# Where the side sums of the modulation vector run in a one-core two-block kernel

## The chip, the cores and the metric

One core of one Trainium2 chip runs the whole program. The metric is the device time of one execution in microseconds (us); the time before is the median of three executions. The engines are named as in the profile: PE is TensorE's matmul, PEld its weight load, DVE is VectorE, ACT is ScalarE, POOL is GpSimd, and SP is the queue from which nearly all DMA loads are issued, in program order.

## What is computed

The reference is a stack of two layers over 256 tokens of width 2048: an RWKV-7 mixer with a convolutional feed-forward, then a layer with windowed attention, a gated recurrence and an MLP. What the change touches is the modulation vector of the first layer:

```python
mod = jax.nn.silu(c) @ ada_w + ada_b                       # (2048) @ (2048, 6*2048)
sh_m, sc_m, g_m, sh_f, sc_f, g_f = jnp.split((mod + ada_table[layer])[:, None, :], N_MOD, axis=-1)
h = _rms(x, norm_mix_pre[layer]) * (1 + sc_m) + sh_m
y, v_first = _rwkv7_mix(h, ...)                            # ends with y @ w_o
x = x + g_m * _rms(y, norm_mix_post[layer])
h = _rms(x, norm_ffn_pre[layer]) * (1 + sc_f) + sh_f
f = _conv_ffn(h, ...)
```

`sh_m` and `sc_m` are needed at the very start. The columns of `g_m`, `sh_f` and `sc_f` (3 x 2048) are needed only at the end of the mixer; they are the work that moves.

## The kernel before

All weights come from HBM as 128x1024 blocks of 32-bit floats (512 KB). Each is loaded by SP into one of three `raw` buffers, split by ACT (high part, L183) and DVE (low part, L184) into one of three pairs of `spl` buffers, and used by PE in three matmuls per product. Every engine works its instructions off in program order, SP too, so an instruction that waits holds everything behind it on its engine.

The columns of `g_m`, `sh_f`, `sc_f` are computed on DVE, as side work. A **sum** is one unit of `ada_sums`: a 128x1024 block of the transposed `ada_w` (half of the 2048 rows for 128 columns) is loaded from `in_adat` by SP (512 KB), and one DVE instruction (L507, `scalar_tensor_tensor` with an accumulator) multiplies it with a row buffer `sb` and adds it up. `sb` holds `silu(c)` for one half of the rows, broadcast over the partitions. When the half changes, `ada_sums` takes two steps without a sum: POOL loads the row (L497), then ACT takes a tanh (L500) and DVE multiplies (L501). `ada_sums` is a generator: each `next` or `pump` in the code around it takes one step, and the load of a later unit is issued inside a step. With `nb` buffers, step n issues the load of unit n+nb-1 at the latest; with one buffer the next load follows the sum that frees the buffer:

```python
load(n + nb)
t = bufs[n % nb]
nc.vector.scalar_tensor_tensor(out=t, in0=t, scalar=0.5, in1=sb, op0=ALU.mult, op1=ALU.mult,
                               accum_out=self.asum[:, h, ch:ch + 1])
if nb == 1 and n + 1 < len(units) and units[n + 1][0] == h:
    load(n + 2)
```

96 units are due before the end of the mixer, in this order: 16 of half 0, 16 of half 1, 32 of half 0, 32 of half 1. The stages that they can lie in, in program order:

- **Mixes** (`mixes`, 174 to 220 us): twelve blocks of the receptance product and then four of the key product. A call site for sums is there, with four buffers, but `N0 = 0` gives it no unit.
- **Scan loop** (`jit`, 220 to 628 us): eight groups of four heads, PE products of key and value with the chunked recurrence (streams `s0`, `s1`, `s2`) between. Units run at fixed slots `SLOT3` (nine per group, four in the first), with a single buffer. The 62 units of `N3` and three changes of half need 68 steps; there are 67 slots. `for _ in s3: pass` takes what is left after the loop.
- **Output product** (`wo`, then `wo_tail`, 628 to 802 us): `y @ w_o` in two halves of 1024 columns, p = 0 and p = 1. Each half takes twelve weight blocks in `wo`, with the recurrence of the last two groups (`s2`) between; four blocks of each half follow in `wo_tail`, the last four (`we`) with their own buffers. The remaining 34 units run here with three buffers, one step or two per weight block (`self.pump(1 + kc % 2)`), 18 steps in each half and the rest in `wo_tail`, where `self.drain()` ends them before `ada_cols` uses the sums.
- The feed-forward runs 32 more units of its own (`gate_f`), which the change doesn't touch.

Of the kernel before, what the change touches and what calls it, by code (L numbers as in the profile page):

```python
# [9 lines left out]
F32 = mybir.dt.float32  # L10
# [87 lines left out]
class Kern:  # L98
# [6 lines left out]
    PSH = [9, 12, 16, 20, 28]  # L105
    LAG = 0
    ASH = [4, 7, 9, 10]
    N0 = 0
    N3 = 62
    SLOT3 = [7, 12, 18, 25, 30, 33, 40, 51, 63]  # L110

    def __init__(self, ctx, tc, A, phases):
# [365 lines left out]
            nc.tensor.matmul(ps[:, j:j + 1], lhsT=acc[:, j * 128:j * 128 + 128], rhs=self.c("ones")[:, 0:1],  # L478
                             start=False, stop=(j == 3))

    def ada_sums(self, units, sb, bufs):


        nc = self.nc
        nb, nxt = len(bufs), 0

        def load(end):
            nonlocal nxt
            while nxt < min(end, len(units)):
                h, ch = units[nxt]  # L490
                nc.sync.dma_start(out=bufs[nxt % nb], in_=self.A["adat"][h, ch])
                nxt += 1
        load(nb - 1)
        half = None
        for n, (h, ch) in enumerate(units):
            if h != half:
                nc.gpsimd.dma_start(out=sb, in_=self.A["rows"][4, h * 1024:h * 1024 + 1024].partition_broadcast(128))  # L497
                yield
                t = bufs[(n + nb - 1) % nb]
                nc.scalar.activation(out=t, in_=sb, func=AF.Tanh, scale=0.5)  # L500
                nc.vector.scalar_tensor_tensor(out=sb, in0=t, scalar=1.0, in1=sb, op0=ALU.add, op1=ALU.mult)  # L501
                half = h
                load(n + nb)
                yield
            load(n + nb)
            t = bufs[n % nb]
            nc.vector.scalar_tensor_tensor(out=t, in0=t, scalar=0.5, in1=sb, op0=ALU.mult, op1=ALU.mult,  # L507
                                           accum_out=self.asum[:, h, ch:ch + 1])
            if nb == 1 and n + 1 < len(units) and units[n + 1][0] == h:
                load(n + 2)  # L510
            yield
# [328 lines left out]
    def mixes(self, xr):  # L840

        nc, wk, hid = self.nc, self.wk, self.hid

        def hidden(i, p, func, scale):
            t = wk.tile([128, S], F32, tag="lt", bufs=2, name="lt")
            nc.scalar.activation(out=t, in_=p, func=AF.Tanh, scale=scale) if func else nc.scalar.copy(out=t, in_=p)
            if scale == 0.5:
                nc.vector.tensor_scalar(out=t, in0=t, scalar1=0.5, scalar2=0.5, op0=ALU.mult, op1=ALU.add)
            self.hilo(hid[:, i, 0, :], hid[:, i, 1, :], t)
        sums = self.ada_sums(self.aunits[:self.N0], wk.tile([128, 1024], F32, name="sb")[:],  # L850
                             [wk.tile([128, 1024], F32, name=f"ab{i}")[:] for i in range(4)])
        self.aunits = self.aunits[self.N0:]
        next(sums, None)
        for i in range(4):
            self.deferred.append(lambda i=i: hidden(i, self.lb[i // 2][:, i % 2, :], i != 1, 1.0 if i < 2 else 0.5))
        ps = [self.bank(b, (128, S), "r") for b in (7, 0, 1, 2, 3, 4)]
        for half in range(2):
            for n, ft in enumerate(range(10, 16)):
                hi, lo = self.wnext()
                for k in range(8):  # L860
                    kc = half * 8 + k
                    w = slice(k * 128, k * 128 + 128)
                    x = xr[:, :, kc, :]
                    nc.tensor.matmul(ps[n][:], lhsT=hi[:, w], rhs=x[:, 0, :], start=(kc == 0), stop=False)
                    nc.tensor.matmul(ps[n][:], lhsT=hi[:, w], rhs=x[:, 1, :], start=False, stop=False)
                    nc.tensor.matmul(ps[n][:], lhsT=lo[:, w], rhs=x[:, 0, :], start=False, stop=(kc == KD - 1))
                    if k == 3:
                        self.flush()
                    if k == 5 and n:
                        self.pump()  # L870
                    if k in (1, 4) and n + half:
                        next(sums, None)
                if half:
                    self.deferred.append(lambda n=n, ft=ft: nc.scalar.copy(out=self.r[:, ft, :], in_=ps[n][:]))
            self.drain()
            self.side = [self.shift_mix(2, xr, range(half * 4, half * 4 + 4))]
        for _ in sums:
            pass
        p = self.bank(5, (128, 2, S), "k")
        for i in range(2):  # L880
            self.feat(p[:, i, :], self.xk, 1, 4)
        self.drain()
        self.flush()
        self.k0 = p
        nc.scalar.preload_act_table_set("natural_log_exp_and_others")
        self.xv = xr
# [58 lines left out]
    def jit(self):  # L945
        nc = self.nc
        self.miscb, self.nmisc = [3, 4, 7], 0
        self.strm, self.due = {}, {}
        self.gr = {}
        self.chain = self.ydone = self.kdone = -1  # L950
        nb = 0

        def nextbank(name):
            nonlocal nb
            nb += 1
            return self.bank((nb - 1) % 3, (128, 2, S), name)
        self.wlate = True
        n3 = self.N3
        ab = self.sp.tile([128, 2, 1024], F32, name="ab")
        s3 = self.ada_sums(self.aunits[:n3], ab[:, 0, :], [ab[:, 1, :]])  # L960
        self.aunits = self.aunits[n3:]
        for g in range(8):
            f = self.gr[g] = {}
            j = 0

            def pump():
                nonlocal j
                for n in ("s2", "s1", "s0"):
                    self.step(n, j)
                if j in self.SLOT3:  # L970
                    next(s3, None)
                j += 1

            def product(n, x):
                p = nextbank("p" + n)
                for i in range(2):
                    self.feat_p(p[:, i, :], x, pump)

                def ev():
                    t = f[n] = self.T([128, 2, S], n)  # L980
                    nc.scalar.copy(out=t, in_=p[:])
                self.deferred.append(ev)
            if g:
                product("k", self.xk)
            else:
                f["k"] = self.T([128, 2, S], "k")
                nc.scalar.copy(out=f["k"], in_=self.k0[:])
                j = 32

            hi, lo = self.wnext()  # L990
            for n, o, ci in (("w", 0, 0), ("a", 256, 1)):
                p = nextbank("z" + n)
                self.lowrank(p, hi, lo, o, (ci,))
                self.flush()

                def ev(p=p, n=n, q=ci):
                    t = f[n] = self.T([128, 2, S], "z" + n)
                    for i in range(2):
                        nc.scalar.activation(out=t[:, i, :], in_=p[:, i, :], func=AF.Tanh, scale=0.5,
                                             bias=self.half[:, q, 2 * g + i:2 * g + i + 1])  # L1000
                self.deferred.append(ev)
            if g > 1:
                p = nextbank("zg")
                self.lowrank(p, hi, lo, 512, (2, 3))
            self.flush()
            if g > 1:
                self.gate(g - 2, p)
            self.strm["s0"] = self.s0(g)
            product("v", self.xv)
            self.finish_stream("s0", "s1", "s2")  # L1010
            self.flush()
            if g:
                self.strm["s2"] = self.s2(g - 1)
            self.strm["s1"] = self.s1(g)
        for _ in s3:
            pass
        self.wlate = False
        self.wo()
# [285 lines left out]
    def wo(self):  # L1304
# [6 lines left out]
        self.G, self.part = sc[:, 0:D], sc[:, D:2 * D].rearrange("p (t c) -> p t c", t=2)  # L1311
        v = [sc[:, 2 * D + i * 1024:2 * D + i * 1024 + 1024] for i in range(4)]
        self.norm_row(self.G, 0)
        self.side = [self.ada_sums(self.aunits, v[0], v[1:4])] if "ffn" in self.phases else []
        gate = self.ada_gate(0, "b_gm", "t_gm", self.G, self.Af[:], lambda: self.misc((128, 4, 128), "gr"))
        next(gate)
        acc = self.acc = {}
# [10 lines left out]
        for p in range(2):  # L1328
# [6 lines left out]
            for kc in range(12):  # L1335
                if p == 0 and kc < 11:
                    split(kc + 1)
                hi, lo = self.wnext()
                self.pump(1 + kc % 2)
                if p == 0 and kc % 2 and kc < 8:  # L1340
                    next(gate, None)
                for tb in range(2):
# [12 lines left out]
                self.strm["s2"] = self.s2(7)  # L1355
            for kc in (12, 13) if p == 0 else (14, 15):
                split(kc)

    def wo_tail(self, wk):
        nc, A = self.nc, self.A  # L1360
# [2 lines left out]
        m = self.ntail = 4  # L1363
        self.wtail(self.tail_o, wk.tile([128, m, 2, 1024], F32R, name="we"))
        for kc in range(12, KD):
            self.pump()
            hi, lo = self.wnext()
            self.tok_mm(acc, hi, lo, (yhl[:, 0, kc, :], yhl[:, 1, kc, :]), kc, (0, 1), False, kc == KD - 1, (2, 3))
            if kc == 13:
# [2 lines left out]
        for tb in range(2):  # L1372
            for i in range(2):
                acc[tb, i] = self.bank(4 + tb * 2 + i, (128, 512), "wo")
        self.drain()
        gain = shift = None
        if "ffn" in self.phases:
            self.ada_cols()
# [527 lines left out]
```

## Time and profile before

| | |
|---|---|
| median of three executions | 2753.27 us (2752.15 to 2753.98) |
| the profiled execution | 2759.31 us, its span 2757.5 us |
| PE, PEld busy | 95%, 86% of the span |
| DVE, ACT busy | 64%, 49% of the span |
| DMA | 534.13 MB, mean 194 GB/s |

PE is the engine that sets the time in most of the program. What a change of other engines' work is worth is therefore read from the stretches in which PE waits, and from the clock that it was granted there.

### The profile page before, as it was taken

How to read it: one execution, taken by the hardware profiler on the slowest of the kernel's cores; microseconds unless marked ns; L12 is line 12 of the kernel's file. 1: busy time of each engine (PE TensorE's matmuls, PEld its weight loads, DVE VectorE, ACT ScalarE, POOL GpSimd, SP SyncE). 2: the span in 40 equal slices, each digit the busy share in tenths (PEclk: the TensorE clock that was granted, in tenths of full speed). 3: DMA queues.
4: the chain of work that ended last, by engine and by line, in shares of the span. 5: the costliest groups of instructions: out<-in, count | busy, mean ns of one | idle time of the engine just before them, and what ended most of it. 6: DMA issues, size and time to landing. Idle time of an engine off the chain costs nothing.

```text
span 2757.5 us, 47818 instructions
## 1 busy us (share of the span) xinstructions
PE 2608.1 (95%) x19345; PEld 2377.1 (86%) x19345; DVE 1775.8 (64%) x2845; ACT 1346.5 (49%) x2206; POOL 61.6 (2%) x101
## 2 busy tenths in 40 slices
PE   6997999998879999999999989999989999999998
PEld 5997788886559999999888789998789999988887
DVE  5977888887567786666555556665554444555555
ACT  3245565664355444444444555655454444444444
POOL 0000111110000000000000000000000000000000
PEclk8999999999889999999999999999999999999999
DMA  8946555556656775555555544443535555556555
GB/s 326 389 145 200 191 191 185 192 182 205 223 193 240 271 268 187 183 183 184 176 194 194 176 155 145 139 139 122 192 131 184 183 183 183 183 191 194 195 192 159
DMA packets 151516, 534.13 MB, mean 194 GB/s; under 512 B 21376, under 2 KB 21760, under 8 KB 150272
## 3 DMA queue, kind: packets, MB, share of 16 engines
q1 hardware_dynamic: 146640, 515.36, 55.7%
q0 software_dynamic: 4368, 13.64, 1.9%
q8 instruction: 151, 2.47, 0.4%
q10 hardware_dynamic: 288, 2.10, 0.2%
q14 instruction: 69, 0.57, 0.1%
HBM read 524.73 MB, written 6.29 MB: 193 GB/s over the span
## 4 chain that ended last, share of the span: by engine, by line
PE 82%; DVE 6%; ACT 6%; DMA 5%; issue 2%; SPq 0%; DVEq 0%; ACTq 0%; POOLq 0%
PE ta L353 7%; PE ta L354 7%; PE ta L352 7%; PE f L276 6%; PE f L274 6%; PE f L275 6%; PE u L276 4%; PE u L275 4%; PE u L274 4%; PE m L1043 3%; PE m L1044 3%; PE m L1045 3%; DMA scratch<-in_adat 2%; PE r L776 2%; DVE spl L184 1%
## 5 line engine op out<-in xcount | busy, mean ns | idle before, releaser
L184 DVE TENSOR_TENSOR spl<-raw,spl 128x1024 fp32r<-128x1024 f32 x748 | 913.1, 1221 | 778.0 <-ACT spl L183 773.6
L183 ACT CAST spl<-raw 128x1024 fp32r<-128x1024 f32 x748 | 782.0, 1046 | 856.8 <-PE ta L354 307.2
L276 PE MATMUL f<-yhl,spl 128*128 128x256 f32 x1376 | 389.5, 283 | 0.4 <-DVE spl L184 0.4
L274 PE MATMUL f<-yhl,spl 128*128 128x256 f32 x1376 | 389.8, 283 | 0.0
L275 PE MATMUL f<-yhl,spl 128*128 128x256 f32 x1376 | 389.4, 283 | 0.0
L352 PE MATMUL ta<-spl,shl 128*128 128x512 f32 x832 | 324.6, 390 | 3.4 <-ACT shl L287 3.4
L353 PE MATMUL ta<-spl,shl 128*128 128x512 f32 x832 | 324.5, 390 | 1.5 <-DVE spl L184 1.5
L354 PE MATMUL ta<-spl,shl 128*128 128x512 f32 x832 | 324.4, 390 | 0.0
L274 PE MATMUL u<-hl,spl 128*128 128x256 f32 x1024 | 289.9, 283 | 0.0
L276 PE MATMUL u<-hl,spl 128*128 128x256 f32 x1024 | 289.8, 283 | 0.0
L275 PE MATMUL u<-hl,spl 128*128 128x256 f32 x1024 | 289.8, 283 | 0.0
L276 PEld LDWEIGHTS f<-yhl,spl 128*128 128x128 f32 x1376 | 264.2, 192 | 0.6 <-DVE spl L184 0.6
L275 PEld LDWEIGHTS f<-yhl,spl 128*128 128x128 f32 x1376 | 264.2, 192 | 0.0
L274 PEld LDWEIGHTS f<-yhl,spl 128*128 128x128 f32 x1376 | 264.2, 192 | 0.0
L1043 PE MATMUL m<-hl,spl 128*128 128x256 f32 x672 | 199.6, 297 | 0.0
L274 PEld LDWEIGHTS u<-hl,spl 128*128 128x128 f32 x1024 | 196.6, 192 | 0.0
L275 PEld LDWEIGHTS u<-hl,spl 128*128 128x128 f32 x1024 | 196.6, 192 | 0.0
L276 PEld LDWEIGHTS u<-hl,spl 128*128 128x128 f32 x1024 | 196.6, 192 | 0.0
L1044 PE MATMUL m<-hl,spl 128*128 128x256 f32 x672 | 189.9, 283 | 0.0
L1045 PE MATMUL m<-hl,spl 128*128 128x256 f32 x672 | 189.8, 282 | 0.0
L352 PEld LDWEIGHTS ta<-spl,shl 128*128 128x128 f32 x832 | 156.6, 188 | 36.6 <-ACT shl L287 3.8
L353 PEld LDWEIGHTS ta<-spl,shl 128*128 128x128 f32 x832 | 156.6, 188 | 34.5 <-DVE spl L184 2.1
(422 smaller groups left out, 4809.8 us busy)
## 6 DMA issues: line engine op xcount, KB each, us to landing
raw<-in_ffn_in SPq DMA_DIRECT2D x172, 512.0 KB, 4.7
raw<-in_w_up SPq DMA_DIRECT2D x128, 512.0 KB, 3.7
raw<-in_w_down SPq DMA_DIRECT2D x128, 512.0 KB, 4.0
raw<-in_ffn_out SPq DMA_DIRECT2D x86, 512.0 KB, 3.8
raw<-in_w_in SPq DMA_DIRECT2D x84, 512.0 KB, 3.7
raw<-in_w_rkv SPq DMA_DIRECT2D x76, 512.0 KB, 4.5
scratch<-in_adat SPq DMA_DIRECT2D x66, 512.0 KB, 5.9
ada<-in_ada SPq DMA_DIRECT2D x64, 512.0 KB, 6.7
```

What stands on the lines that cost most here:

```text
L183: self.nc.scalar.copy(out=hi[:, :n], in_=t[:, :n])
L184: self.nc.vector.tensor_tensor(out=lo[:, :n], in0=t[:, :n], in1=hi[:, :n].bitcast(F32), op=ALU.subtract)
L274: nc.tensor.matmul(out, lhsT=hi[:, w], rhs=xhl[:, 0, kc, :], start=(kc == 0), stop=False)
L275: nc.tensor.matmul(out, lhsT=hi[:, w], rhs=xhl[:, 1, kc, :], start=False, stop=False)
L276: nc.tensor.matmul(out, lhsT=lo[:, w], rhs=xhl[:, 0, kc, :], start=False, stop=(kc == KD - 1))
L352: nc.tensor.matmul(o, lhsT=shl[0][:, t0], rhs=hi[:, w], start=first, stop=False)
L353: nc.tensor.matmul(o, lhsT=shl[0][:, t0], rhs=lo[:, w], start=False, stop=False)
L354: nc.tensor.matmul(o, lhsT=shl[1][:, t0], rhs=hi[:, w], start=False, stop=last)
L776: nc.tensor.matmul(out, lhsT=wd[:, w], rhs=xt[:, g % 2, max(0, min(3, ft - 9)), kc % 2, :], start=False, stop=e)
L1043: nc.tensor.matmul(out, lhsT=hi[:, w], rhs=xhl[:, 0, kc, :], start=(kc == 0), stop=False)
L1044: nc.tensor.matmul(out, lhsT=hi[:, w], rhs=xhl[:, 1, kc, :], start=False, stop=False)
L1045: nc.tensor.matmul(out, lhsT=lo[:, w], rhs=xhl[:, 0, kc, :], start=False, stop=(kc == KD - 1))
```

## The change

Nothing is computed that was not computed before. Three things move:

1. Ten units go to the mixes stage (`N0 = 10`), with its four buffers; the steps there are at k == 1 of each block, and at k == 5 of blocks 3, 4 and 5 of the first half.
2. The scan loop gets 64 units (`N3 = 64`) and now holds four changes of half, so 72 steps for the same 67 slots.
3. The 22 units that are left for the output product are all of half 1. They go on using the row buffer of the scan loop (`half=1`), with five buffers (its block buffer is the fifth), and each step issues the load of the unit three ahead (`lag=1`) after all five were loaded at the first. Beside p = 0 there are four steps, at kc = 2, 5, 8 and 11; beside p = 1 the eighteen as before; none in `wo_tail`.

```diff
-    N0 = 0
-    N3 = 62
+    N0 = 10
+    N3 = 64
...
-    def ada_sums(self, units, sb, bufs):
+    def ada_sums(self, units, sb, bufs, half=None, lag=0):
...
-        load(nb - 1)
-        half = None
+        load(nb if half is not None else nb - 1)
...
-            load(n + nb)
+            load(n + nb - lag)
...
-                    if k in (1, 4) and n + half:
+                    if k == 1 or (k == 5 and not half and n > 2):
                         next(sums, None)
...
-        ab = self.sp.tile([128, 2, 1024], F32, name="ab")
+        ab = self.ab = self.sp.tile([128, 2, 1024], F32, name="ab")
...
-        self.side = [self.ada_sums(self.aunits, v[0], v[1:4])] if "ffn" in self.phases else []
+        self.side = [self.ada_sums(self.aunits, self.ab[:, 0, :], v + [self.ab[:, 1, :]], 1, 1)]
...
-                self.pump(1 + kc % 2)
+                self.pump(1 + kc % 2 if p else kc % 3 == 2)
...
+        self.drain()
...
         for kc in range(12, KD):
-            self.pump()
...
-        self.drain()
         gain = shift = None
```

How it moves instructions, at three places.

DVE where the scan loop ends and the output product begins (L507 is a sum; L1294 to L1299 the end of a group's recurrence; L516 to L518 the gate's columns; L184 a weight split; L288 the split of the product's input). Before:

```order
L507 SCALAR_TENSOR_TENSOR ab,asum<-ab 128x1024
L1294 TENSOR_TENSOR r<-r,Y 128x512
L1297 SCALAR_TENSOR_TENSOR r<-r,vec,bv 128x256
L1299 SCALAR_TENSOR_TENSOR r<-r,vec,zg 128x256
L1297 SCALAR_TENSOR_TENSOR r<-r,vec,bv 128x256
L1299 SCALAR_TENSOR_TENSOR r<-r,vec,zg 128x256
L507 SCALAR_TENSOR_TENSOR ab,asum<-ab 128x1024
L516 TENSOR_TENSOR Af<-asum 128x16
L517 TENSOR_TENSOR Af<-Af,vec 128x16
L518 TENSOR_TENSOR Af<-Af,vec 128x16
L184 TENSOR_TENSOR spl_6673<-raw_6528,spl_6672 128x1024
L288 TENSOR_TENSOR yhl<-r,yhl 128x256 x2
```

And of the change:

```order
L507 SCALAR_TENSOR_TENSOR ab,asum<-ab 128x1024
L1294 TENSOR_TENSOR r<-r,Y 128x512
L1297 SCALAR_TENSOR_TENSOR r<-r,vec,bv 128x256
L1299 SCALAR_TENSOR_TENSOR r<-r,vec,zg 128x256
L1297 SCALAR_TENSOR_TENSOR r<-r,vec,bv 128x256
L1299 SCALAR_TENSOR_TENSOR r<-r,vec,zg 128x256
L507 SCALAR_TENSOR_TENSOR ab,asum<-ab 128x1024 x5
L516 TENSOR_TENSOR Af<-asum 128x16
L517 TENSOR_TENSOR Af<-Af,vec 128x16
L518 TENSOR_TENSOR Af<-Af,vec 128x16
L184 TENSOR_TENSOR spl_6703<-raw_6550,spl_6702 128x1024
L288 TENSOR_TENSOR yhl<-r,yhl 128x256 x2
```

Where one sum stood between the loop and the product, five stand in a row, all on the single buffer.

SP near the end of the output product (L491 is the load of a unit, L492 in the change; `in_w_o` are the product's weight blocks, `in_ffn_in` the next stage's). Before:

```order
L167 DMA raw_7758<-in_w_o 128x1024
L491 DMA scratch<-in_adat 128x1024
L167 DMA raw_7793<-in_w_o 128x1024
L491 DMA scratch<-in_adat 128x1024 x2
L167 DMA raw_7815<-in_w_o 128x1024
L491 DMA scratch<-in_adat 128x1024
L167 DMA raw_7835<-in_w_o 128x1024
L491 DMA scratch<-in_adat 128x1024 x2
L167 DMA raw_7868<-in_w_o 128x1024
L167 DMA raw_7891<-in_w_o 128x1024
L167 DMA raw_7895<-in_w_o 128x1024
L167 DMA raw_7899<-in_ffn_in 128x1024
```

And of the change:

```order
L492 DMA ab<-in_adat 128x1024
L167 DMA raw_7798<-in_w_o 128x1024
L492 DMA scratch<-in_adat 128x1024 x2
L167 DMA raw_7820<-in_w_o 128x1024
L167 DMA raw_7839<-in_w_o 128x1024
L167 DMA raw_7869<-in_w_o 128x1024
L167 DMA raw_7891<-in_w_o 128x1024
L167 DMA raw_7895<-in_w_o 128x1024
L167 DMA raw_7899<-in_ffn_in 128x1024
```

The last five weight blocks follow each other; before, units stood between all but the last three.

ACT where the mixes stage begins (L833 empties five of PE's result banks, L846 is the first of the small functions behind it). Before:

```order
L183 CAST spl_1411<-raw_1240 128x1024
L833 COPY r<-r_257 128x512
L833 COPY r<-r_258 128x512
L833 COPY r<-r_259 128x512
L833 COPY r<-r_260 128x512
L833 COPY r<-r_261 128x512
```

And of the change:

```order
L183 CAST spl_1415<-raw_1240 128x1024
L500 ACT_TABLE_LOAD
L500 ACTIVATE ab_1404<-sb 128x1024
L833 COPY r<-r_257 128x512
L833 COPY r<-r_258 128x512
L833 COPY r<-r_259 128x512
L833 COPY r<-r_260 128x512
L833 COPY r<-r_261 128x512
```

A tanh of 1024 columns now stands ahead of the copies, and the table load that L846 had is now L500's.

## Rows read from the trace of the kernel before

**Rows 1.** The page, part 4: the chain that ended last, by line.

```profile
PE ta L353 7%; PE ta L354 7%; PE ta L352 7%; PE f L276 6%; PE f L274 6%; PE f L275 6%; PE u L276 4%; PE u L275 4%; PE u L274 4%; PE m L1043 3%; PE m L1044 3%; PE m L1045 3%; DMA scratch<-in_adat 2%; PE r L776 2%; DVE spl L184 1%
```

**Rows 2.** Stretches: length, busy time (instructions) by engine, PE clock, DMA share, GB/s.

```profile
174.00:220.00 46.00, 43.31 (x347) 42.90 (x346) 30.66 (x45) 25.75 (x39) 0.00 (x0) 0.96 0.48 160
...
644.00:650.00 6.00, 6.00 (x79) 5.22 (x78) 4.88 (x9) 1.62 (x3) 0.55 (x1) 0.72 0.24 84
...
712.00:718.00 6.00, 4.32 (x13) 3.15 (x13) 5.54 (x9) 3.09 (x5) 0.00 (x0) 0.72 0.40 123
718.00:738.00 20.00, 14.83 (x181) 11.60 (x182) 14.24 (x21) 4.36 (x5) 0.00 (x0) 0.99 0.85 295
738.00:755.00 17.00, 16.60 (x103) 10.70 (x102) 5.44 (x8) 4.39 (x14) 0.00 (x0) 0.51 0.45 149
...
788.00:796.00 8.00, 6.14 (x15) 4.85 (x16) 6.44 (x8) 1.05 (x1) 0.00 (x0) 0.57 0.43 141
```

**Rows 3.** PE's waits, 620 to 850 us: in total us, times, longest.

```profile
PE wo L353 <- DVE spl L184: 8.9, 3, 5.5
PE wo L354 <- DVE yhl L288: 6.3, 3, 3.7
PE ch L1253 <- DVE Pm L1234: 4.0, 1, 4.0
...
PE mi L1141 <- DVE scratch L538: 2.6, 2, 1.7
...
PE mi L1214 <- DVE Tm L1231: 1.1, 1, 1.1
...
PE wo L353 <- DVE we L184: 0.8, 1, 0.8
```

**Rows 4.** Tile `scratch` (units of the output product): what its idle engine waited for.

```profile
DMA scratch<-in_adat: 18.6, 10
```

**Rows 5.** End of the scan loop, timelines of SP, DVE, PE: start, us, instruction.

```profile
622.99 0.33 SPq L491 DMA_DIRECT2D ab<-in_adat  x1
...
628.82 1.23 DVE L507 SCALAR_TENSOR_TENSOR ab<-ab 128x1024 f32<-128x1024 f32 x1 [2.42 <-DMA ab<-in_adat]
629.97 0.08 DVE L507 DVE_READ_ACCUMULATOR ab<-ab 128x1 f32 x1
...
632.11 0.79 PE L354 MATMUL wo<-spl,yhl 128*128 128x512 f32 x1 [3.73 <-DVE yhl L288]
```

**Rows 6.** Tile `ab` (units of the scan loop): min/median/max ns, then landing times.

```profile
L507 DVE SCALAR_TENSOR_TENSOR ab<-ab x62: 1206/1220/1228, 238.6 to 628.8; 128x1024 f32<-128x1024 f32 x62
...
L500 ACT ACTIVATE ab<-ab x3: 1055/1055/1057, 231.1 to 441.7; 128x1024 f32<-128x1024 f32 x3
...
DMA to landing us min/median/max: 3.2/3.7/6.1
```

**Rows 7.** The chain, 220 to 300 us: start, us, what.

```profile
245.48 3.46 DMA ab<-in_adat
...
250.22 4.30 DMA ab<-in_adat
```

**Rows 8.** DVE and PE timelines at 269 and 273 us.

```profile
269.22 1.23 DVE L507 SCALAR_TENSOR_TENSOR ab<-ab 128x1024 f32<-128x1024 f32 x1
...
272.64 0.58 PE L1045 MATMUL pv<-mx,spl 128*128 128x256 f32 x1 [5.95 <-DVE spl L184]
```

**Rows 9.** Begin of the mixes stage, timelines of ACT and PE.

```profile
171.01 2.53 ACT L833 COPY r<-r 128x512 f32<-128x512 f32 x5
173.56 1.28 ACT L846 ACT_TABLE_LOAD   x1
...
179.58 0.38 PE L864 MATMUL r<-mx,spl 128*128 128x256 f32 x1 [1.93 <-ACT spl L183]
```

**Rows 10.** DVE in the second half of the output product.

```profile
735.82 1.23 DVE L507 SCALAR_TENSOR_TENSOR scratch<-scratch 128x1024 f32<-128x1024 f32 x1 [2.29 <-DMA scratch<-in_adat]
```

**Rows 11.** ACT near the end of the output product.

```profile
793.58 1.05 ACT L183 CAST we<-raw 128x1024 fp32r<-128x1024 f32 x1 [6.29 <-DMA raw<-in_w_o]
```

## The prediction

> **What bounds the kernel now.** I read the page first, for what the chain of waits names. It is PE nearly everywhere, and one entry that no PE work explains: the loads of units for the output product, 2% of the span [rows 1]. Then the tile view of those units: ten times an engine was idle until such a load landed, 18.6 us in all [rows 4]. That engine is DVE, and DVE works in order, so behind each late sum stand the weight split or the recurrence step that PE waits for. PE's own waits over the output product and the tail behind it show which [rows 3]; each is read as a DVE instruction that was late. Last the stretches, for the clock granted [rows 2]: PE runs at 2.4 GHz (1.00) except behind such waits, where stretches stand at 0.51 to 0.72, that is partly or wholly at the lower level of 1.2 GHz. So the output product pays twice, with waits and with clock.
>
> The change adds no instruction to DVE: 128 sums stay 128, and seven tanh steps stay seven. What it does is a matter of places, and I price it place by place.
>
> **A. Five sums between loop and product.** 72 steps meet 67 slots, so five units are left when the loop ends, where one is left now. They share one buffer: load, sum, load, sum. Nothing hides them. DVE's next instructions are the gate columns, the split of the first weights and of the product's input, and PE already waits for these: 3.73 us until 632.11, behind the one sum that waited 2.42 us for its load [rows 5]. SP is held too: the row for the gate and the third weight block stand behind the five loads. Two blocks are loaded ahead of these, so I add nothing for them (one landing, 3.7 [rows 6], if that cover is too short). One round is load to sum 3.46 us and sum to next load 1.28 us, from 245.48 to 250.22 [rows 7]: 4.74 us. The first of the five gains 1.5 us, since its load has no weight load beside it: it waited until 628.82 for a load issued at 622.99 [rows 5], and needs 3.46 to 4.3 us by itself [rows 7]. Four more rounds, 19.0, less 1.5: about +17. Bounds: the shortest landing, 3.2 [rows 6], in place of 3.46 gives +16; rounds as long as the one at 622.99 (5.83 + 1.28 = 7.1, four of them) give +28.
>
> **B. Ten sums in the mixes stage.** DVE is busy 30.66 of 46 us there [rows 2]; ten sums at 1.22 [rows 6] and one multiply of the same shape are 13.4, which fits, but barely. PE was busy 43.31 of 46, so there is little to win. On the path lies the tanh: it comes ahead of the five bank copies on ACT, and ACT leads PE there (the weight split that PE waited 1.93 us for until 179.58 came behind the copies) [rows 9]. The table load of 1.28 [rows 9] only changes its place; the tanh itself is 1.06 [rows 6]. The multiply and the sums behind each split push the second and third split back by about one sum each, within the 3.2 us that PE has for a block there (46 us for 347 recorded matmuls, 24 to a block [rows 2]). Transfers: ten units of 0.524 MB within about 40 us add 131 GB/s to 160, at a share of 0.48 now [rows 2]; 160/0.48 is 333 GB/s at full share, so it holds on average and not in the two blocks where two units and a weight block fall due together. I take +1.5; bounds +1 and +5 (one landing of 3.7 [rows 6] fully exposed on top of the tanh; nothing speaks for a gain).
>
> **C. The scan loop.** The changes of half come at other slots. In the second group the step at 269.22 is no longer a sum but a row load on POOL, and DVE was late there: PE waited 5.95 us for a split that stood behind that sum [rows 8]. This gives back one sum, −1.3 (bounds 0 and −2.5, if the next step's multiply also comes earlier). The other groups have DVE to spare; the two sums that they get cost nothing unless a split falls right behind.
>
> **D. First half of the product.** Fourteen sums and two tanh steps go, four sums stay. The waits that stood behind them are PE's on L538 (the gate's bank), 2.6, and on L288 without the 3.73 of part A, 6.3 − 3.7 = 2.6 [rows 3]. The clock dip 644 to 650 (6 us at 0.72) is 1.7 us lost [rows 2]. Together 6.9. The first sum at kc = 2 stands closely behind its load, five in a burst, so I leave 1 us: −6 (bounds −2 and −8).
>
> **E. Second half of the product.** As many sums as before, eighteen beside twelve blocks, but each load is issued three units ahead and not two, and SP isn't held by the sum just before. Every other weight block takes two steps at once, and then two units ahead were too few: the sum of 735.82 waited 2.29 us [rows 10]. Waits of PE there: the recurrence's Tm, 1.1, and Pm, 4.0, and two of the three splits, 8.9 − 5.5 = 3.4 [rows 3]. Of the 4.0 only the 2.29 is the load; the rest is DVE's own queue. That is 1.1 + 2.3 + 3.4 = 6.8. Clock: 712 to 718, 6 us at 0.72, is 1.7 lost; 738 to 755, 17 us at 0.51, is 8.3 lost [rows 2]. That long dip followed the 4.0 us wait. I take the first whole and the second by half, because 1.7 us of the wait stays and because PE, busy 16.60 of these 17 us, stayed low nonetheless. Together −12.7; bounds −6 (4.5 of waits and the first dip) and −18.6 (all of it).
>
> The Trainium skill (TensorE: Matmul & The Clock Gate, Part 1: The HAM clock gate) says that the clock follows how busy the engine has been lately. By that rule a half without waits keeps the full clock, and the whole 8.3 would come back; the sum would be 4.2 us lower. The rows of 738 to 755 agree with it only in part.
>
> **F. End of the product.** Now SP's last weight blocks stand behind unit loads that wait for sums; PE waited 5.5 for the fifteenth block and 0.8 for `we` [rows 3], ACT up to 6.29 for a block's landing [rows 11], and 788 to 796 (8 us at 0.57) lost 3.4 us of clock [rows 2]. With the units done earlier, five blocks follow each other on SP. 5.5 + 0.8 + 3.4 = 9.7, less 1.7 for blocks that then come at the pace of splits: −8 (bounds −4 and −9.7).
>
> **Sum.** +17 + 1.5 − 1.3 − 6 − 12.7 − 8 = −9.5. The terms are of the profiled execution, 2759.31 us (2757.5 of span and 1.8 around it), which is 6.0 above the median of 2753.27; none of them scales with that difference, so I carry −9.5 over: 2743.8, **2744 us**.
>
> **Rivals.**
> 1. *The second half keeps its pace; slower.* Eighteen sums beside twelve blocks remain, and 718 to 738 ran at a DMA share of 0.85 [rows 2]. If it is transfers that make the sums late, more buffers only lengthen the queue: E gives nothing and F its lower bound, 17 + 1.5 − 1.3 − 6 − 4 = +7.2, 2760.5. It decides as soon as E and F together fall below 5.7. Against it: share 0.45 right behind, at 149 GB/s [rows 2]. Chance 0.17. The Trainium skill (DMA: Bandwidth & Descriptors, Specifications) gives a limit of about 358 GB/s from HBM for a core; an estimate by it is 29 blocks of 0.524 MB in 42 us, well inside the 76 us from 712 to 788, which speaks against this rival.
> 2. *All the clock comes back.* E and F at their bounds and D at −6.9: 17 + 1.5 − 1.3 − 6.9 − 18.6 − 9.7 = −18, 2735. Chance 0.17. The Trainium skill's rule on the clock, named under E (TensorE: Matmul & The Clock Gate, Part 1), would lead here.
> 3. *The five sums take longer.* At A's upper bound, if these loads land as late as the last one did: 28 − 26.5 = +1.5, 2755. For: that row. Against: the weight loads that ran beside it are now held behind the five. Chance 0.10.
> 4. *The mixes stage chokes.* B at +5: −6, 2747. Chance 0.10.
>
> **How the numbers follow.** The forecast has 0.46. A measurement of this kernel can tell about 0.2% (5.5 us) from no change, so faster means below 2747.8 and slower above 2758.8. Faster: 0.43 of the forecast (its own range is 2739 to 2750), all of rival 2, half of rival 4: 0.65. Slower: 0.11 of rival 1 and 0.02 of rival 3: 0.13. Same: 0.22. The range leaves out the far ends of rivals 1 and 2: 2733 to 2760.
>
> **What would show it.** A: five sums in a row on DVE, four more loads of `ab` of 3.4 to 3.6 us each in the chain, and a PE wait on L288 near 20 us. B: PE's wait for the bank copies (L833) longer by 2.3, the one at 179.58 shorter, the stage 1 to 2 us longer. C: the 5.95 at 4.7. D and E: no sum that waits over 1 us for its load, and PEclk 1.00 where 738 to 755 was. F: no wait of 5 us at the fifteenth block. I would be wrong if the waits of E come back on other DVE instructions (then late splits are DVE's own load, not the transfers'), or if PE's wait at A is far from 20.

## The result, and the profile of the changed kernel

The change made the kernel slower: 2771.7 us in the median of four runs (2768.36 to 2776.38), against 2753.62 us before; the ratio is 1.0064 (1.0049 to 1.0079). I had forecast 2744 and given 0.13 to slower; the range ended at 2760. The profiled execution took 2768.36 us, its span 2766.2 us.

The first reading is where the span grew. The tile views list for each line of code its first and last start. The tiles `r` (product of the mixes stage), `pv` (the scan loop's value product) and `wo` (the output product) give the borders of three stages; this is the changed kernel.

```profile
L864 PE MATMUL r<-mx,spl x96: 277/283/582, 164.1 to 218.1; 128*128 128x256 f32 x96
L1043 PE MATMUL pv<-mx,spl x256: 278/283/1202, 231.4 to 636.1; 128*128 128x256 f32 x128
L1045 PE MATMUL pv<-mx,spl x256: 277/283/581, 231.6 to 636.4; 128*128 128x256 f32 x128
L354 PE MATMUL wo<-spl,yhl x112: 387/390/793, 661.6 to 805.7; 128*128 128x512 f32 x112
```

From the first start of L864 to the first of L1043 is the mixes stage; to the last of L1045 the scan loop; to the last of L354 the product without its last four weight blocks. The same rows of each profiled kernel:

| us | mixes | scan loop | product | median of the runs |
|---|---|---|---|---|
| before | 54.5 | 401.9 | 174.7 | 2753.6 |
| after | 67.3 | 405.0 | 169.3 | 2771.7 |
| tanh late | 60.1 | 406.1 | 168.8 | 2764.0 |
| row first | 64.9 | 406.7 | 169.3 | 2767.2 |
| mixes alone | 68.2 | 402.9 | 167.0 | 2764.0 |
| tenth slot | 67.0 | 435.7 | 147.0 | 2773.6 |
| no sums between (and tanh late) | 60.4 | 405.3 | 157.6 | 2746.9 |
| primed loads | 67.8 | 404.0 | 159.8 | 2760.5 |
| five buffers alone | 54.5 | 401.8 | 147.8 | 2737.0 |
| five buffers again | 53.0 | 403.5 | 152.5 | 2733.9 |
| four buffers alone | 54.5 | 404.0 | 152.3 | 2739.9 |
| all mended | 59.1 | 408.7 | 143.0 | 2732.7 |

Before to after: mixes +12.8, loop +3.1, product −5.4. The mixes stage began 2.5 us earlier in this execution, and the rest is 0.7 longer; that is the +8.7 of the two spans. The two profiled executions lie on the wrong sides of their medians (before 5.7 us above, after 3.3 below), which makes the 18 us of the medians. Why other executions of the changed kernel took up to 8 us more isn't shown, since one was profiled. How far one profiled execution can be trusted is seen where the same kernel was profiled twice: five buffers alone and again differ by 1.5 us in the mixes stage, 1.7 in the loop and 4.7 in the product. Smaller differences between rows of the table say nothing by themselves.

**The mixes stage.** PE's waits of the changed kernel, 140 to 225 us (total, times, longest):

```profile
PE r L864 <- ACT r L833: 12.1, 1, 12.1
PE r L866 <- DVE spl L184: 4.4, 4, 1.9
```

And of the kernel before, by the same view:

```profile
PE r L864 <- ACT spl L183: 1.9, 1, 1.9
PE r L864 <- ACT r L833: 1.9, 1, 1.9
PE r L866 <- DVE spl L184: 0.8, 1, 0.8
```

The wait for the bank copies (L833) grew from 1.9 to 12.1 us. Timelines of POOL and ACT at this place:

```profile
169.06 0.66 POOL L497 DMA_DIRECT2D sb<-in_rows  x1 [168.60 <-DVE mx L700]
...
167.62 1.04 ACT L183 CAST spl<-raw 128x1024 fp32r<-128x1024 f32 x1
176.58 1.28 ACT L500 ACT_TABLE_LOAD   x1 [7.92 <-issue]
177.87 1.06 ACT L500 ACTIVATE ab<-sb 128x1024 f32<-128x1024 f32 x1
178.83 2.52 ACT L833 COPY r<-r 128x512 f32<-128x512 f32 x5
```

And the landing of that row, in the view of the tile `sb`:

```profile
DMA to landing us min/median/max: 7.4/7.4/7.4
```

ACT is idle from 168.66 to 176.58 with no releaser that the profile names; 169.06 and 7.4 us of landing make 176.5. The tanh waits for its row, and the five copies that free PE's banks stand behind it. The idle time of 7.92 us, the table load of 1.28 and the tanh of 1.06 are together 10.3 us, which is within 0.1 us what the wait grew by. The row itself was issued no earlier, because POOL waited for DVE's last L700.

**The sums between loop and product** came as priced. DVE (the second and third of the five) and PE timelines:

```profile
644.50 1.22 DVE L507 SCALAR_TENSOR_TENSOR ab<-ab 128x1024 f32<-128x1024 f32 x1 [3.40 <-DMA ab<-in_adat]
...
648.95 1.23 DVE L507 SCALAR_TENSOR_TENSOR ab<-ab 128x1024 f32<-128x1024 f32 x1 [3.21 <-DMA ab<-in_adat]
...
661.62 0.79 PE L354 MATMUL wo<-spl,yhl 128*128 128x512 f32 x1 [19.35 <-DVE yhl L288]
```

**Beside the product** most of the waits of [rows 3] are gone: no split lets PE wait over 0.9 us (8.9 in three waits before), and the 4.0 for Pm and the 2.6 for L538 are not in the list any more. What the change left or brought, 635 to 860 us, is the wait just shown and one for Tm. Behind the Tm wait stands DVE's first sum of the product, which waited for its load; all five loads had been issued only then:

```profile
PE wo L354 <- DVE yhl L288: 19.4, 1, 19.4
...
PE mi L1141 <- DVE Tm L1231: 5.7, 1, 5.7
...
PE wo L353 <- DVE spl L184: 0.9, 1, 0.9
```

```profile
682.66 1.22 DVE L507 SCALAR_TENSOR_TENSOR scratch<-scratch,ab 128x1024 f32<-128x1024 f32 x1 [5.75 <-DMA scratch<-in_adat]
...
677.32 2.00 SPq L492 DMA_DIRECT2D scratch<-in_adat  x4
```

The stretches show the clock that answers to [rows 2]: low behind the two waits, full in the second half (1.00 in every stretch from 712 to 804).

```profile
663.00:672.00 9.00, 9.00 (x60) 6.54 (x59) 4.28 (x8) 2.60 (x4) 0.00 (x0) 0.76 0.40 127
...
684.00:690.00 6.00, 5.33 (x20) 4.82 (x21) 3.96 (x7) 1.72 (x3) 0.00 (x0) 0.50 0.49 196
...
750.00:770.00 20.00, 19.18 (x197) 13.64 (x195) 14.47 (x23) 6.83 (x15) 0.00 (x0) 1.00 0.93 336
770.00:784.00 14.00, 13.60 (x114) 8.43 (x108) 7.18 (x10) 7.45 (x20) 0.00 (x0) 1.00 0.58 196
784.00:798.00 14.00, 14.00 (x63) 11.37 (x62) 12.11 (x19) 7.11 (x9) 0.00 (x0) 1.00 0.71 240
```

### The profile page after: what moved, and what is told of

It is laid out like the page before. It is cut to its first block, busy times and chain, and to the rows that moved or that the text cites. A ratio compares the mean times of both kernels' runs of the same rounds, so it can differ in the third digit from the quotient of the medians.

```text
span 2766.2 us, 47819 instructions
## 1 busy us (share of the span) xinstructions
PE 2607.1 (94%) x19345; PEld 2378.3 (86%) x19345; DVE 1776.6 (64%) x2845; ACT 1344.7 (49%) x2205; POOL 61.5 (2%) x101
## 4 chain that ended last, share of the span: by engine, by line
PE 84%; DVE 6%; ACT 5%; DMA 3%; issue 2%; SPq 0%; DVEq 0%; ACTq 0%; POOLq 0%
PE ta L353 7%; PE ta L352 7%; PE ta L354 7%; PE f L276 6%; PE f L274 6%; PE f L275 6%; PE u L276 4%; PE u L274 4%; PE u L275 4%; PE m L1043 3%; PE m L1044 3%; PE m L1045 3%; PE r L776 1%; PE mi L1141 1%; DVE spl L184 1%
## 5 line engine op out<-in xcount | busy, mean ns | idle before, releaser
L184 DVE TENSOR_TENSOR spl<-raw,spl 128x1024 fp32r<-128x1024 f32 x748 | 913.1, 1221 | 766.5 <-ACT spl L183 761.8
L354 PE MATMUL ta<-spl,shl 128*128 128x512 f32 x832 | 323.7, 389 | 0.0
L1043 PE MATMUL m<-hl,spl 128*128 128x256 f32 x672 | 199.5, 297 | 0.0
L1045 PE MATMUL m<-hl,spl 128*128 128x256 f32 x672 | 189.8, 282 | 0.0
```

What stands on the lines that cost most here:

```text
L184: self.nc.vector.tensor_tensor(out=lo[:, :n], in0=t[:, :n], in1=hi[:, :n].bitcast(F32), op=ALU.subtract)
L354: nc.tensor.matmul(o, lhsT=shl[1][:, t0], rhs=hi[:, w], start=False, stop=last)
L1043: nc.tensor.matmul(out, lhsT=hi[:, w], rhs=xhl[:, 0, kc, :], start=(kc == 0), stop=False)
L1045: nc.tensor.matmul(out, lhsT=lo[:, w], rhs=xhl[:, 0, kc, :], start=False, stop=(kc == KD - 1))
```

## The experiments

**1. The tanh one block later** (on the changed kernel).

```diff
-                    if k == 1 or (k == 5 and not half and n > 2):
+                    if (k == 1 and n + half) or (k == 5 and not half and n > 2):
```

> The changed kernel, with the tanh of the mixes stage one weight block later, behind the five bank copies and the small functions. Theory 1: PE's 12.1 us wait for the bank copies comes from the row that the tanh needs, which landed 7.4 us after its issue at 169.06; with the tanh behind the copies this wait goes to about 2 us and the time to about 2762 us (9 to 10 us less than the changed kernel). Rival: ACT and the two engines behind it then wait for the row or for splits a block later, and the time stays within 3 us of 2771.7.

2763.95 us (1.0034, 1.0021 to 1.0047). ACT does the copies first, and the row lands under them and the small functions, though it takes 7.9 us:

```profile
169.66 2.52 ACT L833 COPY r<-r 128x512 f32<-128x512 f32 x5
...
178.09 1.05 ACT L500 ACTIVATE ab<-sb 128x1024 f32<-128x1024 f32 x1
```

PE's wait for the copies is 1.9 us again. Theory 1 holds: taking this wait away gave back 7.8 us of the loss, a little less than the 9 to 10 I had expected. The stage is still 5.6 us longer than before; splits behind sums make PE wait 4.8 us, where it was 0.8.

**2. The units of the mixes stage alone** (on the kernel before).

```diff
-    N0 = 0
-    N3 = 62
+    N0 = 10
+    N3 = 52
...
-                    if k in (1, 4) and n + half:
+                    if k == 1 or (k == 5 and not half and n > 2):
```

> The kernel before, with ten units in the mixes stage as in the change and 52 in the scan loop; the output product is that of before. Theory 1: the mixes stage alone costs 10 to 13 us, so 2763 to 2767 us, with a PE wait of 12 us for the bank copies. Forecast of the prediction (terms B and C): +0.2, 2754. Rival: the loss of the change lies in the output product, and this kernel stays within 3 us of 2753.6.

2763.96 us (1.0031, 1.0019 to 1.0042), with a wait of 12.6 us for the copies. The mixes stage alone costs some 9 us of the median (the kernel before, run beside it, took 2754.6), and its stage is 13.7 longer. The product is 7.7 us shorter in this execution: no sum is left between loop and product here, and PE's waits for L288 fell from 6.3 us to 2.9; the rest isn't traced.

**3. A tenth slot in the scan loop** (on the changed kernel).

```diff
-    SLOT3 = [7, 12, 18, 25, 30, 33, 40, 51, 63]
+    SLOT3 = [7, 12, 18, 22, 25, 30, 33, 40, 51, 63]
```

> The changed kernel, with a tenth slot for sums in each group of the scan loop (22 beside 7, 12, 18, 25, ...), so that no sum is left between the loop and the product. Term A of the prediction priced the five sums at 17 us: then about 2755 us, with PE's wait for L288 near zero. Rival: the scan loop has no room for five more rounds of 4.7 us on one buffer, PE waits there for splits behind sums, and half is given back: about 2763 us.

2773.62 us (1.0064, 1.0048 to 1.0081): no gain, a miss. But the parts are clear. The product is 22 us shorter, and the loop 31 us longer; its PE waits, 228 to 640 us:

```profile
PE ch L1253 <- DVE Pm L1234: 15.4, 6, 3.1
PE pv L1043 <- ACT k L981: 9.8, 1, 9.8
```

Neither is in the changed kernel's list of the loop's waits. DVE before one of the first, where PE waited 3.01 us until 451.00:

```profile
447.76 1.22 DVE L507 SCALAR_TENSOR_TENSOR ab<-ab 128x1024 f32<-128x1024 f32 x1 [2.59 <-DMA ab<-in_adat]
...
450.16 0.69 DVE L1234 TENSOR_TENSOR Pm<-mi,Pm 128x512 f32<-128x512 f32 x1
```

With one buffer the new slot's sum comes too soon after the one before it, waits for its load, and `Pm` stands behind. The 9.8 us come once, in the second group, and ACT's timeline there shows the same fault as in the mixes stage:

```profile
279.69 1.28 ACT L500 ACT_TABLE_LOAD   x1 [7.73 <-DMA ab<-in_rows]
280.98 1.06 ACT L500 ACTIVATE ab<-ab 128x1024 f32<-128x1024 f32 x1
281.94 1.03 ACT L183 CAST spl<-raw 128x1024 fp32r<-128x1024 f32 x1
282.88 0.58 ACT L981 COPY k<-pk 128x512 f32<-128x512 f32 x1
```

The change of half now falls where the tanh stands ahead of the copy that PE waits for, and the tanh's table load waited 7.73 us for the row. In the changed kernel that copy comes first, at 274.04, and the tanh at 281.17. Besides, the clock is 0.93 to 0.98 from 330 us on, where the changed kernel has 1.00 up to 581. The rival named the place, but not the waits, and its 2763 us are 10 too few. The loop's own loss hides the gain, so this kernel can't price the five sums by itself.

**4. Five buffers alone** (on the kernel before).

```diff
-        ab = self.sp.tile([128, 2, 1024], F32, name="ab")
+        ab = self.ab = self.sp.tile([128, 2, 1024], F32, name="ab")
...
-        self.side = [self.ada_sums(self.aunits, v[0], v[1:4])] if "ffn" in self.phases else []
+        self.side = [self.ada_sums(self.aunits, self.ab[:, 0, :], v + [self.ab[:, 1, :]])] if "ffn" in self.phases else []
```

> The kernel before with one edit: the units of the output product use the row buffer and the block buffer of the scan loop too, so five buffers in place of three; all 34 units and their steps stay. If five buffers are what frees the second half (terms E and F, 20.7 us together), the time goes to about 2735 to 2742 us. Rival: it is the missing units in the first half and at the end that free it, and the time stays within 4 us of 2753.6.

2736.95 us (0.9931, 0.9917 to 0.9945). With all 34 units beside it the product takes 147.8 us here and 152.5 when the kernel was profiled again, about as much as with 22 of them and no sums in front (147.0, experiment 3). DVE's wait for the units of the product, 620 to 770 us, and two stretches:

```profile
DVE scratch L507 <- DMA scratch<-in_adat: 1.8, 1, 1.8
```

```profile
700.00:720.00 20.00, 18.64 (x193) 15.02 (x191) 18.95 (x31) 10.30 (x16) 0.00 (x0) 1.00 0.99 357
720.00:740.00 20.00, 19.19 (x205) 12.54 (x204) 10.55 (x16) 8.52 (x25) 0.00 (x0) 1.00 0.72 256
```

The 18.6 us of [rows 4] have become 1.8, and the clock is full in both stretches. The transfers filled the DMA engines for 20 us, with a share of 0.99 at 357 GB/s, and PE was busy 18.64 of these 20 us all the same. The Trainium skill (DMA: Bandwidth & Descriptors, Specifications) gives a core about 358 GB/s from HBM; this stretch agrees with it as a mean over 20 us, while slices of 0.35 us in the changed kernel's mixes stage reached 468.

**5. No sums between loop and product** (on the kernel of experiment 1).

```diff
-    N3 = 64
+    N3 = 59
...
-                self.pump(1 + kc % 2 if p else kc % 3 == 2)
+                self.pump(1 + kc % 2)
```

> The kernel with the late tanh, and with the five sums between loop and product undone in another way than a tenth slot: 59 units in the scan loop (67 steps for 67 slots), 27 beside the product, with one or two steps at each weight block in both halves as before the change. If the five sums cost what term A says (17 us) or what the tenth-slot kernel's product says (22 us shorter), the time goes from 2764 to 2742 to 2747 us, and the scan loop stays as long as with the late tanh (406 us), so that the loop's loss with the tenth slot was that slot's. Rival: the product can't carry five more sums in the first half; PE waits return there and the time stays above 2752 us.

2746.92 us (0.9975, 0.9963 to 0.9987): 17.0 us less than experiment 1, as term A has it, with the loop at 405.3 us: the loop's loss in experiment 3 was that slot's. PE's waits for L288 are down to 1.0 us. The experiment isn't A alone: five more units lie beside the product, and the steps of its first half are spaced otherwise. (The profiled execution, 4.7 us above the median, shows a product 11.2 us shorter; DVE waited 11.6 us there for the loads of sums, up to 6.8 at once.)

**6. Four buffers alone** (on the kernel before; the block buffer `ab[:, 1, :]` is the fourth).

```diff
-        self.side = [self.ada_sums(self.aunits, v[0], v[1:4])] if "ffn" in self.phases else []
+        self.side = [self.ada_sums(self.aunits, v[0], v[1:4] + [self.ab[:, 1, :]])] if "ffn" in self.phases else []
```

> The kernel before with one edit: four buffers in place of three for the units of the output product. Five gave 2737 us. If the gain comes from a load that is issued three units ahead of its sum (as the change's lag leaves it), four buffers give most of it: 2736 to 2742 us. Rival: the transfers need the deepest queue that there is, and four buffers give half: about 2745 us.

2739.9 us (0.9947, 0.9930 to 0.9963). DVE's waits for these loads are 5.0 us, with three buffers 18.6. The fourth buffer gives most; what the fifth adds, 3 us, lies inside the two intervals.

**7. The row first** (on the changed kernel).

```diff
-        load(nb if half is not None else nb - 1)
+        load(nb if half is not None else nb - 1 if nb < 4 else 0)
```

> The changed kernel, where the three unit loads that SP issues with the row load of the mixes stage come only after the tanh. Theory 1a: the row lands late (7.4 us) because 1.5 MB of units and a weight block move beside it; alone it lands in 4 to 5 us, PE's wait for the bank copies falls from 12.1 to 9 us, and the time by 1 to 3 us, since the first sums then wait instead. Rival 1b: the 7.4 us are the row's own, and the wait stays within 1 us of 12.1.

2767.19 us (1.0048, 1.0033 to 1.0063), 4.5 us less than the changed kernel where I had expected 1 to 3; the two intervals overlap. The row's landing in the tile view of `sb`, then ACT's tanh and SP's issues:

```profile
DMA to landing us min/median/max: 4.7/4.7/4.7
```

```profile
175.12 1.06 ACT L500 ACTIVATE ab<-sb 128x1024 f32<-128x1024 f32 x1
...
169.87 0.33 SPq L167 DMA_DIRECT2D raw<-in_w_rkv  x1
170.30 7.49 SPq L492 DMA_DIRECT2D ab<-in_adat  x4
```

The row lands in 4.7 us in place of 7.4, and PE waits 9.4 in place of 12.1. But the edit doesn't do what I wrote: the unit loads come behind the tanh in the code, yet SP doesn't wait for ACT, and three of them go out at 170.3, 170.7 and 171.2, before the tanh. The row isn't alone; it is ahead. In the changed kernel the units are issued at 168.5, 168.9 and 169.4, around the row's 169.06. The queue of the row (q0) shows what that makes. Packets, MB and share of each queue in the changed kernel, 168.5 to 172.3 us and then 172.3 to 176.6:

```profile
q1 hardware_dynamic: 255, 0.98, 73.4%
...
q1 hardware_dynamic: 237, 0.84, 51.9%
q0 software_dynamic: 144, 0.52, 44.5%
```

For 3.2 us after its issue no byte of the row moved, while 0.98 MB of other loads did. With the row first its queue begins at 170.3 us, 1.3 after the issue. So theory 1a holds in a narrower form: of the 7.4 us, 2.7 come from the unit loads being issued around the row and not behind it, and most of that is lost before the row's first byte. Why the row's queue got nothing in that time isn't shown.

The Trainium skill (DMA: Bandwidth & Descriptors, Anatomy of one DMA) counts some 2.0 us fixed and the bytes at 436 GB/s. An estimate by it is 3.2 us for the row by itself and 6.8 us for four transfers of 0.524 MB in the time of one. The measured 4.7, with other loads behind the row, and 7.4, with a weight block besides the units, are both longer; no run here has the row alone.

**8. The product's first loads issued two blocks ahead** (on the changed kernel).

```diff
         load(nb if half is not None else nb - 1)
+        if half is not None:
+            yield
...
-                self.pump(1 + kc % 2 if p else kc % 3 == 2)
+                self.pump(1 + kc % 2 if p else kc % 3 == 2 or not kc)
```

> The changed kernel, with the five loads ahead of the product's first sum issued by a step of their own at the first weight block, two blocks ahead of the first sum. Term D left 1 us for that sum standing behind its own load; the trace has 5.75 us of DVE and 5.7 us of PE. If that wait is the burst alone, PE's wait for Tm goes away and the time falls by 5 to 8 us, to about 2765 us. Rival: it moves to the next sum or to the weight blocks that are then behind the burst on SP, and the time stays within 3 us of 2771.7.

2760.46 us (1.0022, 1.0012 to 1.0032), 11 us less, and the product 9.5 us shorter. PE's wait for Tm is gone, and so is the clock dip behind it:

```profile
672.00:684.00 12.00, 12.00 (x147) 9.88 (x145) 9.16 (x14) 3.34 (x6) 0.00 (x0) 1.00 0.44 154
684.00:690.00 6.00, 6.00 (x56) 4.56 (x55) 4.21 (x7) 2.09 (x4) 1.61 (x3) 1.00 0.32 95
```

I had expected 5 to 8; the wait was 5.7, and the 6 us at half the clock that followed it are 3 more.

**9. All three mended, beside five buffers alone.** The edits of experiments 1 and 8, `N3 = 59`, and one step at every block of p = 0 but kc = 1.

> The change with its three faults mended at once: the tanh of the mixes stage one block later, 59 units in the scan loop so that none is left between loop and product, and the product's five loads issued two blocks ahead of its first sum; 27 units beside the product, ten in the mixes stage. If moving units pays at all, this beats five buffers alone (2737 us), since the product has seven units fewer: 2730 us or less. Rival: the product with five buffers had no cost to give back, and the mixes stage (5.6 us longer with the late tanh) and the loop (3 to 4 us longer) are lost: 2740 to 2746 us.

> The kernel before with five buffers alone, once more beside the mended kernel on one chip, for the difference of the two: 2737 us.

2732.66 us (0.9924, 0.9911 to 0.9937) and 2733.91 us (0.9936, 0.9923 to 0.9950). The two can't be told apart: in the profiled executions the mended kernel has the product 9.5 us shorter (143.0 and 152.5), and loses 6.1 in the mixes stage and 5.2 in the loop. Between the theories the answer is in the middle; moving the units pays nothing that can be measured, and five buffers pay nearly all. The three faults add up: 7.8 (experiment 1), 17.0 (5) and 11.2 (8) off 2771.7 make 2735.7, and with all three mended 2732.7 were measured.

## Why the prediction was wrong

**B, the step that failed.** I took +1.5 and let it go to +5; the stage grew by 12.8. I wrote that "on the path lies the tanh" and priced the instruction, 1.06 us, but not what it waits for. The table load and the tanh did cost their 2.3 us; the 7.92 us that ACT stood idle ahead of them were missing. The row is loaded by POOL just ahead, and the only landing that I put into the bound was one of a unit, 3.7. The row landed after 7.4 us, 2.7 of them because the unit loads of the same step were issued around it and not behind it (experiment 7), and it was issued only when POOL's wait for DVE was over. Rival 4 named the place, with less than half the price. Taking the tanh off the path gave back 7.8 us (experiment 1); of the 5.6 us that stay in the stage 4.0 are splits behind sums, which I had let pass because they fit into PE's time for a block on average.

**C.** I took −1.3 and got +3.1. The 5.95 us of [rows 8] did become 4.6, as I said. But the clock was lower in the first two groups, two stretches of 50 us each (0.96 and 0.91 before, by the same view):

```profile
231.00:281.00 50.00, 41.04 (x279) 37.37 (x277) 37.00 (x73) 27.83 (x44) 3.37 (x5) 0.90 0.70 217
281.00:331.00 50.00, 43.69 (x434) 38.73 (x435) 45.95 (x87) 22.54 (x41) 7.01 (x11) 0.86 0.59 189
```

50 × (0.06 + 0.05) are 5.5 us of full pace. What lowered it isn't isolated; no run changed the loop alone. Nor is it sure that the change did: with the loop of before, the second execution of five buffers has 0.91 and 0.88 there and 403.5 us, and four buffers have 404.0. Only some 1 to 3 of the 3.1 us can be put down to the change.

**A** was right: rounds of 4.4 to 5.0 us, PE's wait 19.35 where I had said near 20, and 17.0 us when it was undone, though not by itself (experiment 5). Not counted in it were the 9 us at 0.76 behind the wait (2.2 us).

**D** was mis-sized. For the first sum, which "stands closely behind its load", I left 1 us. All five loads are issued at that sum, behind a weight block; it waited 5.75, with 3 us of clock behind. Experiment 8 gave back 11.

**E and F** were about right: the product's −5.4 less some +17 to +19 for A leaves −22 to −24 for D, E and F, where I had −26.7 with D at −6. With D some 8 us worse than that, E and F gave −24 to −26, between my −20.7 and rival 2's −28.3; the two profiled executions allow no closer reading. No sum after the first waited over 1.1 us, the clock was 1.00 where [rows 2] have 0.51, and no wait of 5 us was left at the fifteenth block. So rival 1 is out, and the clock came back in full in the second half, as rival 2 and the Trainium skill's rule (TensorE: Matmul & The Clock Gate, Part 1: The HAM clock gate) would have it. The prediction doesn't say which part does this; experiment 4 does. It is the buffers: three left a load too little time before its sum, and one more was nearly enough (experiment 6). Taking twelve units away besides cost B and A, and gave nothing that could be measured even with the faults mended (experiment 9, seven units fewer).

In the profiled executions the span grew by 8.7 us where the forecast was −9.5. Against their terms B is 11.3 us worse, C 4.4 and the product (A, D, E and F) 4.3; the mixes stage began 2.5 earlier and the rest is 0.7 longer, which makes these 18.2 us. The other 9 us of the miss in the medians come from where the two profiled executions stand to them, and are not explained.

## What to carry to other kernels

When an instruction is put ahead of others on an engine that works in order, price what it waits for, with the landing of its own load and the loads that are issued around it, and not its own duration alone. Where side work beside a busy stage is late, look first whether its loads are issued early enough: here one or two more buffers were worth 14 to 18 us, and with twelve of the units moved elsewhere besides, the kernel was 35 us slower than that. A stage whose idle engines suggest room on average can still have none at the slot where the work is put.

## What was not expected of the hardware

One wait of PE cost half as much again in clock: 5.7 us of waiting were followed by 6 us at 0.50, and without both the product was 9.5 us shorter. The same 0.5 MB row landed in 4.7 us when three unit loads were issued 1.3 to 2.2 us behind it, and in 7.2 to 8.3 us, over all runs, when they were issued around it.
